# Down projection of 768 tokens by a recursion of seven block products, its sums made in the stage before

## The chip, the cores and the metric

The kernel runs on one core of a Trainium2 chip. The metric is the device time of one execution in microseconds; runs of the same kernel on the same chip are compared by their medians.

## The reference

One decoder layer for a prompt of 1024 tokens and 8 decode tokens that share the weights, all in float32. Columns are tokens: T = 1032. After the branches (RG-LRU, windowed attention, memory attention), a gated merge and an output projection with a layer norm, each token has a vector h of 1024 values. The last part of the layer is

```python
h = layer_norm(ALPHA * x + merged @ w_out, ln1_g, ln1_b)
gt, up = jnp.split(h @ w_gate_up, 2, axis=-1)        # 1024 -> 2 x 2816
h = layer_norm(ALPHA * h + (jax.nn.silu(gt) * up) @ w_down, ln2_g, ln2_b)   # 2816 -> 1024
```

The change is about the last line's product with w_down, 2816 x 1024.

## The kernel before, in words

Every tile has 128 partitions. 2816 = 22 x 128 gives NF = 22 "rows" f of the inner dimension, 1024 = 8 x 128 gives 8 output tiles m. A float32 operand is split into a high part (a cast to fp32r, on ACT) and a low part (the rest, a subtraction on DVE): `split`, lines L81 and L82. A product of two such pairs takes three matmuls, high x high, high x low and low x high, all accumulated in one PSUM bank.

**Gate and up stage** (`units`, `unit_step`). Two of the 22 rows are computed directly (`direct_units`); the other 20 rows are units. A unit multiplies the 2x2 blocks of (gate, up) weights with the 2x2 blocks of h by a recursion of seven products instead of eight: steps i = 0 to 6. The weight sums are made by VectorE just ahead (`fast_quarter`, L284, three steps ahead of TensorE), the sums of h once before (`h_sums`, tiles h_, t). A step is 24 matmuls of 258 columns: 4 row tiles x 3 x 2 halves p. Banks: fb (three rooms of tag mm), fd (t), fc (s). Evictions: ACT copies (L1188, L1190), then VectorE (L1192, L1195, L1197, L1199, L1200, L1202) and a tanh (L1198) make the activated row ft, and SP stores it to DRAM, tensor scr_f (L1204). SP also loads the gate and up weights (wgu, L92) into six rooms of tag raw.

**Down stage** (`down`). The tokens are in three chunks CH: 384, 384 and 264 (256 prompt and 8 decode tokens). For each chunk and each output tile m, `streamed` runs over the 22 rows: weights wdn are loaded by SP in pieces of four tiles, split (wd_h, wd_l), and used in three matmuls per row (L1244, L1245, L1246) into a bank dl. The rows are read back from scr_f by POOL's queue (`rows`, L1253, tiles gl and gh) and split. The first twelve rows of the first chunk are multiplied for four output tiles before the rest. Each finished bank is added to ALPHA x residual by VectorE (L1300, tile acc), summed for the mean, and the layer norm of a chunk (`layer_norm`, L961 to L977) runs in steps beside the next chunk's products (`norm_step`, at the output tiles in NORM_AT). The third chunk ends in `last_layer_norm`, which is the end of the kernel; its outputs o_y are stored by SP (L1290).

**Order.** The program is written as one stream; a list scheduler sets the order on each engine's queue, by readiness in its own model of times and then by place in the program. Each engine executes its queue in order. Memory of a closed pool is used again by the next one, and an instruction that writes there waits for the last user of the old tile.

Of the kernel before, what the change touches and what calls it, by code (L numbers as in the profile page):

```python
# [10 lines left out]
F32 = mybir.dt.float32  # L11
# [7 lines left out]
P = 128  # L19
# [5 lines left out]
CH = ((0, 384), (384, 384), (768, 264))  # L25
# [4 lines left out]
DIRECT_AT = ((0, 258), (258, 258), (516, 252), (768, 264))  # L30
ROOMS = (*range(83, 67, -1), *range(36, 4, -1), *range(67, 36, -1), *range(4, -1, -1))
EARLY, EARLY_ROWS = ("mm", "s", "mm", "s"), 12
# [26 lines left out]
class Builder:  # L59
# [218 lines left out]
    def fast_quarter(self, st, i):  # L278

        nc, ((a11, a12), (a21, a22)), u = self.nc, st["raw"], st["u"]  # L280
        if i in (1, 2, 4, 5):
            src = self.w1.tile([P, D // 2], F32, tag="sum", name=f"us{u}_{i}", bufs=self.sums)
# [659 lines left out]
    def col_mean(self, s, n, name):  # L942

        nc = self.nc
        hi = self.ph.tile([P, 384], F32R, tag="lh", name=f"{name}h", bufs=1)[:, :n]
        lo = self.ph.tile([P, 384], F32R, tag="ll", name=f"{name}l", bufs=1)[:, :n]
        self.split(hi, lo, s)
        ps = self.bank("o", f"{name}p")[:, :n]
# [4 lines left out]
    def layer_norm(self, c, r, s1, gcol, emit, name, late=False):  # L953
# [5 lines left out]
        mu = self.col_mean(s1, n, f"{name}mu{c}")  # L959
        s2 = ph.tile([P, 384], F32, tag="s2", name=f"{name}s2{c}", bufs=1)[:, :n]  # L960
        for m in range(KT):  # L961
            nc.vector.tensor_sub(r[m], r[m], mu)
            sq = s2 if m == 0 else ph.tile([P, 384], F32, tag="sq", name=f"{name}sq{c}_{m}", bufs=2)[:, :n]
# [5 lines left out]
        var = self.col_mean(s2, n, f"{name}va{c}")  # L969
        rs = ph.tile([P, 384], F32, tag="s2", name=f"{name}rs{c}", bufs=1)[:, :n]  # L970
# [20 lines left out]
    def last_layer_norm(self, n, r, product, gcol, emit):  # L991
# [4 lines left out]
        tile_ = lambda tag, name, bufs, dt=F32: ph.tile([P, 384], dt, tag=tag, name=name, bufs=bufs)[:, :n]  # L996
        s1, s2 = tile_("s1", "ls1", 1), tile_("s2", "ls2", 1)
        hi, lo = (ph.tile([P, n], F32R, tag=f"c0{e}", name=f"c0{e}", bufs=1) for e in "hl")
        e1, e2 = self.bank("t", "le1")[:, :n], self.bank("t", "le2")[:, :n]
# [13 lines left out]
        for m in range(KT):  # L1013
            ps = product(m, last=m < LATE)
# [6 lines left out]
            if m == 1:  # L1021
                s = tile_("xres", "lc0", 3)
                nc.vector.tensor_add(s, r[0], r[1])
                self.split(hi, lo, s)
            elif m == LATE - 1:
                with self.tc.issue_after(self.last_mm):
                    c0 = self.bank("o", "c0")[:, :n]
# [11 lines left out]
        mu, rs = tile_("xres", "lmu", 3), tile_("gt", "lrs", 3)  # L1039
# [481 lines left out]
```

## Time and profile before

| | |
|---|---|
| median of 3 runs | 1949.3 us (1948.71 to 1951.92) |
| span of the profiled execution | 1949.3 us, clock 0.997 |
| gate and up units | about 1280 to 1682 us |
| down, chunks of 384 tokens | 1682 to 1866.5 us |
| down, chunk of 264 tokens | 1866.5 to 1935 us |
| tail | 1935 to 1949.3 us |

In the profile, a busy time is a union of instruction times; matmuls overlap, so their distance of starts, not their duration, is what one costs. DVE is VectorE, ACT ScalarE, PE TensorE, POOL GpSimd and SP the queue that issues most DMAs. An "idle before" is charged to what ended the wait.

### The profile page before, as it was taken

The page shows a single profiled execution, that of the slowest core. Times are in us where ns is not written, and L with a number is a line of the kernel's source. Part 1 is how long each engine was busy: PE and PEld are TensorE (multiplying, and loading weights), DVE is VectorE, ACT ScalarE, POOL GpSimd, SP SyncE. Part 2 cuts the span into 40 slices and gives each one's busy share as a digit, 9 for nine tenths or more (in the row PEclk, how much of TensorE's full clock was granted, in tenths as well). Part 3 has the DMA queues.
Part 4 walks back from the last instruction along what each step waited for, and adds up shares of the span by engine and source line. Part 5 has one row for each costly group of instructions (what it writes and reads, how often), then busy time and mean ns, then how long its engine had stood idle before and what let it go on. Part 6 is the DMA issues. An engine that isn't in the chain of part 4 may idle for free. (4 is left out here: it accounts for less than half of the span.)

```text
span 1949.3 us, 37970 instructions
## 1 busy us (share of the span) xinstructions
PE 1912.5 (98%) x14356; PEld 1880.8 (96%) x14356; DVE 1364.0 (70%) x2875; ACT 1013.5 (52%) x2198; POOL 141.9 (7%) x218
## 2 busy tenths in 40 slices
PE   8999999999999999999999999999999999999997
PEld 8999999999999999989999999999999999999997
DVE  8678887888777555379877557976565665757566
ACT  5465565465556445378775245643333333635444
POOL 1000000000011200012210000000000000402002
PEclk9999999999999999999999999999999999999999
DMA  7444545365323866567534341122222222846554
GB/s 231 145 164 147 171 166 183 128 216 168 130 90 137 275 213 206 156 169 221 157 88 154 118 142 44 45 75 99 78 87 88 87 82 71 279 131 190 155 159 139
DMA packets 170919, 281.92 MB, mean 145 GB/s; under 512 B 20864, under 2 KB 85456, under 8 KB 170704
## 3 DMA queue, kind: packets, MB, share of 16 engines
q1 hardware_dynamic: 165840, 264.72, 43.0%
q0 software_dynamic: 4896, 14.78, 2.3%
q8 instruction: 112, 1.84, 0.4%
q14 instruction: 71, 0.58, 0.1%
HBM read 214.64 MB, written 66.85 MB: 144 GB/s over the span
## 5 line engine op out<-in xcount | busy, mean ns | idle before, releaser
L1246 PE MATMUL dl<-gh,wd_l 128*128 128x384 f32 (+1 forms) x528 | 167.4, 317 | 3.0 <-DVE wd_l L82 3.0
L1244 PE MATMUL dl<-gh,wd_h 128*128 128x384 f32 (+1 forms) x528 | 167.0, 317 | 1.0 <-ACT gh L81 1.0
L1245 PE MATMUL dl<-gl,wd_h 128*128 128x384 f32 (+1 forms) x528 | 167.2, 317 | 0.0
L1246 PEld LDWEIGHTS dl<-gh,wd_l 128*128 128x128 f32 x528 | 99.0, 188 | 3.5 <-DVE wd_l L82 3.5
L1244 PEld LDWEIGHTS dl<-gh,wd_h 128*128 128x128 f32 x528 | 98.9, 188 | 1.3 <-ACT gh L81 1.3
L1245 PEld LDWEIGHTS dl<-gl,wd_h 128*128 128x128 f32 x528 | 99.0, 188 | 0.5 <-DVE gl L82 0.5
L1253 POOL DMA_DIRECT2D gl<-scr_f x66 | 35.6, 540 | 789.0 <-PE fb L1179 630.8
L81 ACT CAST u_1h<-us 128x512 fp32r<-128x512 f32 x48 | 29.8, 621 | 87.6 <-issue 43.5
L592 ACT ACTIVATE bp<-bp,bst 128x257 f32<-128x257 f32 (+1 forms) x128 | 62.8, 493 | 18.0 <-DVE bst L588 17.7
L284 DVE TENSOR_TENSOR us<-ur,ur 128x512 f32<-128x512 f32 x96 | 66.0, 688 | 5.0 <-DMA ur<-win 2.9
L81 ACT CAST u_2h<-us 128x512 fp32r<-128x512 f32 x48 | 29.7, 619 | 76.5 <-PE fb L1179 38.2
L284 DVE TENSOR_TENSOR us<-us,ur 128x512 f32<-128x512 f32 x96 | 66.2, 689 | 2.3
L82 DVE TENSOR_TENSOR u_6l<-ur,u_6h 128x512 fp32r<-128x512 f32 x48 | 33.0, 688 | 43.8 <-PE fb L1180 28.5
L115 PE MATMUL brs<-bsH,wbs_h 128*128 128x384 f32 (+1 forms) x192 | 61.0, 319 | 1.0 <-ACT bsH L81 1.0
L82 DVE TENSOR_TENSOR u_4l<-us,u_4h 128x512 fp32r<-128x512 f32 x48 | 33.0, 687 | 40.1 <-PE fb L1180 29.1
L116 PE MATMUL brs<-bsL,wbs_h 128*128 128x384 f32 (+1 forms) x192 | 61.0, 318 | 0.0
L117 PE MATMUL brs<-bsH,wbs_l 128*128 128x384 f32 (+1 forms) x192 | 60.9, 317 | 0.0
L588 DVE CUSTOM_DVE_ANT_0 bp<-bs,mask,nsnk 128x256 f32<-128x256 f32 (+1 forms) x128 | 54.7, 458 | 3.3 <-PE bs L585 2.2
L82 DVE TENSOR_TENSOR u_5l<-us,u_5h 128x512 fp32r<-128x512 f32 x48 | 33.1, 690 | 30.0 <-PE fd L1180 14.6
L1198 ACT ACTIVATE ft<-za 128x516 f32<-128x516 f32 x40 | 25.5, 636 | 52.4 <-DVE za L1197 52.0
L81 ACT CAST u_5h<-us 128x512 fp32r<-128x512 f32 x48 | 30.0, 625 | 38.2 <-DVE us L284 24.7
L81 ACT CAST u_0h<-ur 128x512 fp32r<-128x512 f32 x48 | 29.8, 621 | 38.1 <-PE ub L301 19.2
(2019 smaller groups left out, 8112.7 us busy)
## 6 DMA issues: line engine op xcount, KB each, us to landing
ur<-win SPq DMA_DIRECT2D x112, 256.0 KB
ur<-wgu SPq DMA_DIRECT2D x80, 256.0 KB
scr_f<-ft SPq DMA_DIRECT2D x40, 258.0 KB
gl<-scr_f POOLq DMA_DIRECT2D x44, 192.0 KB, 4.8
dck<-cmk SPq DMA_DIRECT2D x32, 256.0 KB
dcv<-cmvT SPq DMA_DIRECT2D x32, 256.0 KB
st<-scr_q SPq DMA_DIRECT2D x32, 256.0 KB
scr_g<-za SPq DMA_DIRECT2D x10, 516.0 KB
```

Of the source, the lines that this page charges most:

```text
L81: ins = self.nc.scalar.copy(hi, src).ins
L82: self.nc.vector.tensor_sub(lo, src, hi.bitcast(F32))
L115: nc.tensor.matmul(ps, sh, mh, start=i == 0, stop=False)
L116: nc.tensor.matmul(ps, sh, ml, start=False, stop=False)
L117: self.last_mm = nc.tensor.matmul(ps, sl, mh, start=False, stop=closes and i == last).ins
L284: nc.vector.tensor_add(src, a, b)
L588: nc.vector.tensor_tensor_reduce(pg[g], s[:, u * 256:u * 256 + n], msk, 1.0, snk[:, g:g + 1], ALU.add, ALU.min, st[:, g:g + 1])
L592: nc.scalar.activation(x, x, AF.Exp, bias=st[:, g:g + 1], scale=-1.0, accum_out=st[:, 4 + g:5 + g])
L1244: nc.tensor.matmul(ps, sh, mh, start=k == 0, stop=False)
L1245: nc.tensor.matmul(ps, sh, ml, start=False, stop=False)
L1246: self.last_mm = nc.tensor.matmul(ps, sl, mh, start=False, stop=closes and k == NF - 1).ins
L1253: self.nc.gpsimd.dma_start(lo.bitcast(F32), self.scf[f][:, t0:t0 + n])
```

## The change

- The chunks become 384, 390 and 258 for the branch and output projections, and four equal pieces of 258 for the two direct rows. `h_sums` pairs tokens so that half p of a unit holds 516 consecutive tokens; a unit's store to scr_f is then contiguous.
- For the down product the tokens are two halves of 516; the first 384 of each half are the two token blocks of a 2x2 recursion, the last 132 of each half (NC) make one chunk of 264 that is multiplied directly as before. The other 2x2 is over the weights: rows f below and above 11 (KD), output tiles 2j and 2j + 1. Seven products, in the order DOWN_ORDER, each over four pairs j and eleven rows, in pieces of 4, 4 and 3 tiles (DOWN_PIECES).
- Four of the seven products need weight sums and four need row sums. They are made during the gate and up stage: `down_sums` (16 jobs of loads, four adds, stores to scr_w; one job every fourth step) and `row_sums` (once per unit f >= 11; two rows read back from scr_f, two taken from the unit's own ft, four subtractions, stores to scr_s). Both use a pool xs of four scratch tiles.
- In `down`, seven products replace the 16 (chunk, m) products of the two 384 chunks. Four banks b and four banks c hold running sums: products 0, 2, 4, 6 go into b and 3, 1, 5 into c without being cleared where a product adds to an earlier one. A bank is added to or subtracted from the residual after each product (`evict`).
- The norm of the second token block runs beside product 6, that of the first beside the last chunk. Low parts of the unsummed weights of products 0, 3 and 6 stay in memory (KEPT) and are used again for three quarters of the last chunk's weights, where only the high part is cast anew.

```diff
-CH = ((0, 384), (384, 384), (768, 264))
+CH = ((0, 384), (384, 390), (774, 258))
...
+KD = NF // 2
+NA = 384
+NC = T // 2 - NA
+DOWN_ORDER = (0, 3, 2, 1, 5, 4, 6)
+DOWN_PIECES = ((0, 4), (4, 4), (8, 3))
+SUM_PIECES = ((0, 3), (3, 3), (6, 3), (9, 2))
+KEPT = (0, 3, 6)
...
+    def down_sums(self, j, e):
+        nc = self.nc
+        o, n = SUM_PIECES[e][0] * P, SUM_PIECES[e][1] * P
+        a11, a12, a21, a22 = (self.scratch(f"dw{j}{e}{x}", n) for x in range(4))
+        for x, a in enumerate((a11, a12, a21, a22)):
+            at = (x % 2) * KD * P + o
+            nc.sync.dma_start(a, self.io["wdn"][2 * j + x // 2][:, at:at + n])
+        nc.vector.tensor_add(a22, a21, a22)
+        nc.vector.tensor_add(a21, a11, a21)
+        nc.vector.tensor_add(a11, a22, a11)
+        nc.vector.tensor_add(a12, a11, a12)
+        for i, a in ((1, a22), (4, a21), (2, a11), (5, a12)):
+            nc.sync.dma_start(self.scw[j][:, SUM_AT[i], o:o + n], a)
+    def row_load(self, k):
+        x = [self.scratch(f"rx{k}{h}", NA) for h in range(2)]
+        for h in range(2):
+            self.nc.sync.dma_start(x[h], self.scf[k][:, h * HT:h * HT + NA])
+        return x
+    def row_sums(self, k, early, st):
+        nc = self.nc
+        x00, x01 = early
+        x10, x11 = st["t", 0][:, :NA], st["t", 1][:, :NA]
+        t1, t4 = (self.scratch(f"rs{k}{x}", NA) for x in range(2))
+        nc.vector.tensor_sub(t1, x00, x01)
+        nc.vector.tensor_sub(x01, x11, x01)
+        nc.vector.scalar_tensor_tensor(x00, x01, -1.0, x00, op0=ALU.mult, op1=ALU.subtract)
+        nc.vector.scalar_tensor_tensor(t4, x00, -1.0, x10, op0=ALU.mult, op1=ALU.subtract)
+        for i, a in ((1, t1), (4, x01), (2, x00), (6, t4)):
+            nc.sync.dma_start(self.scs[k][:, ROW_AT[i] * NA:(ROW_AT[i] + 1) * NA], a)
...
             self.unit_step(st[f], i)
+            if n % 4 == 0 and jobs:
+                self.down_sums(*jobs.popleft())
+            if i == 3 and f >= KD:
+                early = self.row_load(f - KD)
             if i == 6:
+                if f >= KD:
+                    self.row_sums(f - KD, early, st[f])
                 del st[f]
...
+        for n, i in enumerate(DOWN_ORDER):
+            ahead = deque(range(KD))
+            nxt = [None] * KD
+            for j in range(KT // 2):
+                opens = i in (0, 1, 3)
+                if opens:
+                    tag = ("mm", "mm", "mm", "o")[j] if i == 0 else "st"[j % 2]
+                    banks["b" if i == 0 else "c", j] = self.bank(tag, f"dl{i}_{j}")[:, :NA]
+                ps = banks["b" if i in (0, 2, 4, 6) else "c", j]
+                mm = partial(nc.tensor.matmul, ps, skip_group_check=not opens)
+                for e, (k0, nk) in enumerate(DOWN_PIECES):
+                    wh, wl = self.down_weights(i, j, e)
+                    for k in range(k0, k0 + nk):
+                        w = slice((k - k0) * P, (k - k0 + 1) * P)
+                        xh, xl = act[k]
+                        mm(wh[:, w], xh, start=opens and k == 0, stop=False)
+                        mm(wh[:, w], xl, start=False, stop=False)
+                        self.last_mm = mm(wl[:, w], xh, start=False, stop=k == KD - 1).ins
+                    if ahead:
+                        k = ahead.popleft()
+                        if i == 6:
+                            last[k] = self.last_row(k)
+                        else:
+                            nxt[k] = self.down_row(DOWN_ORDER[n + 1], k, "ba"[n % 2])
+                    if i == 6 and (j, e) in ((0, 2), (1, 1), (2, 0), (2, 2)):
+                        self.norm_step()
+                evict(i, j, ps)
+            act = nxt
+            if i == 4:
+                norm_of(1)
+        norm_of(0)
+        for f in range(KD, NF):
+            last[f] = self.last_row(f)
```

More of the change, by code (lines that the diff above doesn't have):

```diff
@@ L24 @@
 T = TP + NB
-CH = ((0, 384), (384, 384), (768, 264))
+CH = ((0, 384), (384, 390), (774, 258))
+CW = 390
 NM = 256
@@ L1013, in last_layer_norm @@
         for m in range(KT):
-            ps = product(m, last=m < LATE)
+            ps = view(product(m, m < LATE))
             if m in NORM_AT:
@@ new lines, in rooms @@
+    def rooms(self):
+        side = lambda x, ks: [(f"{x}{2 * k + e}", NA) for k in ks for e in range(2)]
+        low = lambda i, js: [(f"k{i}{j}{e}", DOWN_PIECES[e][1] * P) for j in js for e in range(3)]
+        for tag, n in (low(0, (0, 1)) + low(6, (0, 1, 2)) + low(0, (2, 3)) + side("a", range(8, KD)) + low(6, (3,))
+                       + low(3, range(4)) + side("b", range(KD)) + [("pad", 64)] + side("a", range(8))):
+            self.gd.tile([P, n], F32R, tag=tag, name=f"room_{tag}", bufs=1)
@@ new lines, in down, with emit_to, emit @@
+        self.norm, self.lows = None, {}
+        self.rooms()
+        at = (0, HT)
+        r = [[a[:, o:o + NA] for a in self.accs] for o in at]
+        act = [self.down_row(DOWN_ORDER[0], k, "a") for k in range(KD)]
+        banks = {}
+        s1 = [ph.tile([P, CW], F32, tag=f"s1{x}", name=f"o2s{x}", bufs=1)[:, :NA] for x in range(2)]
+        done = [[], []]
+        def emit_to(dst):
+            def emit(m, v, scale=1.0):
+                nc.scalar.activation(v, v, AF.Identity, bias=self.vec[:, V_B2 + m:V_B2 + m + 1], scale=scale)
+                nc.sync.dma_start(dst(m), v)
+            return emit
@@ L1307, in build @@
+        tail = lambda a: a.rearrange("p (q n) -> p q n", q=2)
+        rows = [tail(a)[:, :, NA:] for a in self.accs]
+        self.last_layer_norm(2 * NC, rows, product, V_G2, emit_to(lambda m: tail(io["o_y"][:, m, :])[:, :, NA:]), tail)
     def build(self):
```

218 lines of the change are left out of this document (125 added, 93 removed).

## The prediction

> **What bounds the kernel now.** I read the page first, then its stretches of the second half, then who waited for whom on TensorE.
>
> ```profile
> span 1949.3 us, 37970 instructions
> PE 1912.5 (98%) x14356; PEld 1880.8 (96%) x14356; DVE 1364.0 (70%) x2875; ACT 1013.5 (52%) x2198; POOL 141.9 (7%) x218
> ```
>
> ```profile
> 1272.00:1477.00 205.00, 204.36 (x1706) 204.15 (x1706) 127.74 (x241) 78.02 (x156) 0.00 (x0) 1.00 0.26 84
> 1477.00:1682.00 205.00, 203.31 (x1697) 202.90 (x1695) 123.95 (x235) 77.29 (x154) 11.38 (x21) 1.00 0.33 106
> 1682.00:1774.00 92.00, 92.00 (x528) 91.48 (x529) 57.92 (x111) 47.16 (x98) 20.13 (x38) 1.00 0.61 190
> 1774.00:1866.50 92.50, 92.50 (x536) 92.50 (x535) 57.59 (x106) 43.39 (x84) 4.11 (x8) 1.00 0.55 164
> 1866.50:1935.00 68.50, 65.45 (x539) 64.83 (x538) 50.86 (x92) 36.91 (x71) 6.20 (x6) 1.00 0.55 164
> 1935.00:1949.30 14.30, 2.38 (x13) 1.71 (x12) 7.60 (x14) 5.69 (x12) 3.91 (x5) 0.76 0.22 76
> ```
>
> The columns after the length are PE, PEld, DVE, ACT and POOL busy, granted clock, DMA share, GB/s. TensorE is the bound in every stretch but the last 14.3 us: the gate and up stage (to 1682), the two down passes of 384 tokens (to 1866.5) and the pass of 264 all run at the full clock, with VectorE 60 to 75% busy beside it. TensorE's waits in the two stages are short (total us, times, longest; the first row is gate and up, the others down):
>
> ```profile
> PE fb L1180 <- DVE u_0l L82: 1.3, 2, 0.6
> ```
>
> ```profile
> PE dl L1246 <- DVE wd_l L82: 3.0, 2, 2.2
> PE dl L1244 <- ACT gh L81: 1.0, 1, 1.0
> ```
>
> So a matmul less is worth its full pitch, and work added elsewhere is free until it makes TensorE wait.
>
> **The matmuls removed.** The 768 tokens took 2 passes x 8 output tiles x 22 row tiles x 3 = 1056 matmuls of 384 columns; the recursion takes 7 products x 4 x 11 x 3 = 924. Removed: 132. Busy times overlap, so the price is the distance of starts:
>
> ```profile
> 1829.71 0.33 PE L1246 MATMUL dl<-gh,wd_l 128*128 128x384 f32 x1
> ...
> 1830.23 0.33 PE L1246 MATMUL dl<-gh,wd_l 128*128 128x384 f32 x1
> ```
>
> Three matmuls in 0.52 us, 0.1733 each (the two passes, 184.5 us over 1056 and the norm's 4, give 0.174). 132 x 0.1733: **-22.9 us**. The Trainium skill ("TensorE: Matmul & The Clock Gate", Back-to-back issue gap) puts the gap of a lone warm matmul at N/2.4 + 2.5 ns, 162.5 ns for 384 columns; the estimate by it would be -21.4 us, and the trace's longer pitch decides.
>
> The last 264 tokens keep their 528 matmuls. Chunk widths 390 and 258 replace 384 and 264 in the branch and output projections: equal sums, and a pitch nearly linear in columns (0.12 at 258 in the rows of fb below against 0.1733 at 384, 0.42 ns a column), so **0**. This is TensorE's own time and nothing would cover a difference.
>
> **The sums in the gate and up stage.** 16 jobs of down_sums (four loads, four adds, four stores, one job every fourth step) and 11 of row_sums (two loads, four subtractions, four stores). Twelve jobs have 384 columns, four have 256. VectorE's price for 512 and 384 columns, and the end of a unit on VectorE and on TensorE:
>
> ```profile
> 1681.30 0.68 DVE L82 TENSOR_TENSOR wd_l<-wd_0r__22005,wd_h 128x512 fp32r<-128x512 f32 x1
> 1681.95 2.43 DVE L82 TENSOR_TENSOR gl<-gl,gh 128x384 fp32r<-128x384 f32 x5
> ```
>
> ```profile
> 1637.79 0.70 DVE L1199 SCALAR_TENSOR_TENSOR ft<-ft,za 128x516 f32<-128x516 f32 x1 [0.71 <-ACT ft L1198]
> ...
> 1640.28 0.42 DVE L1202 SCALAR_TENSOR_TENSOR ft<-fb,ft 128x258 f32<-128x258 f32 x1
> ```
>
> ```profile
> 1640.53 0.28 PE L1178 MATMUL fb<-H_0h,u_0h 128*128 128x258 f32 x1
> ...
> 1641.98 0.28 PE L1178 MATMUL fb<-H_0h,u_0h 128*128 128x258 f32 x1
> ```
>
> Five of 384 take 2.43, so 0.47 each (0.35 at 256 in proportion); one of 512 takes 0.65 to the next start. Jobs: 48 x 0.47 + 16 x 0.35 = 28 us over the first 64 of 140 steps; a step is 24 matmuls, twice the 1.45 between the two rows of fb, so 64 steps are 186 us, and VectorE goes there from 62 to 77%. Row sums: 44 x 0.47 = 21 us over the last 220 us, 60 to 70%. The nearest row for such a load is the projection, which runs the same seven products:
>
> ```profile
> 300.00:600.00 300.00, 298.58 (x2455) 297.11 (x2455) 235.02 (x459) 173.53 (x334) 18.84 (x20) 1.00 0.45 152
> ```
>
> VectorE is at 78% and TensorE idle 0.5%, which over 402 us is 2 us against the 1.3 of now. The tight place is the unit's end: the eviction of the first fb bank ends at 1640.70, and the second half of the next unit's first step, which opens that bank again, starts at 1641.98: 1.3 us of cover, with VectorE nearly full before it. Two adds fit, three don't. I take **+1.5**, nearest to the projection's row; ends 0 and 8 (0.4 at each of 20 units).
>
> SP carries 128 + 66 more DMAs, and already waits for VectorE most of this stage:
>
> ```profile
> SPq L92 <- DVE us L284: 145.2, 33, 6.4
> SPq L1204 <- DVE ft L1200: 119.8, 19, 19.2
> ```
>
> That is 265 of 410 us. A sum's store that waits for its add (2 us for a job) holds back the wgu loads queued behind it, but the six raw rooms let those run up to a unit, 20 us, ahead of use: **0**; with that lead gone each would cost its landing. The bytes (w_down read and its sums written, 11.5 MB each, rows 4.3 and 8.7: 36 MB over 400 us, 90 GB/s beside 84 to 106) stay near the 152 that the projection moved. The contiguous scf store and the strided view in h_sums move the same columns under TensorE: **0**, and a few 0.1 us if they came on the path.
>
> **The seam at 1682.**
>
> ```profile
> 1680.64 0.28 PE L1180 MATMUL fb<-h_3h,u_6l 128*128 128x258 f32 x1
> 1681.97 0.62 PE L1244 MATMUL dl<-gh,wd_h 128*128 128x384 f32 x2 [1.05 <-ACT gh L81]
> ```
>
> ```profile
> L1253 POOL DMA_DIRECT2D gl<-scr_f x66: 536/538/595, 1662.9 to 1856.4; - x66
> DMA to landing us min/median/max: 2.7/4.3/5.4
> ```
>
> TensorE waits 1.05 us for the first cast rows, and will again: eleven rows come early as twelve did. New is a room. By the sizes in the code the kept low parts of product 0's first weights lie where the scratch of the sums lay, and the last unit's row_sums store from it. The last three subtractions follow the last eviction (three times 0.47, done near 1682.8), then SP's stores land. The trace shows no landing of an SP store; POOL's row loads took 2.7 to 5.4, so the first low parts can be written at about 1686 to 1688. Two of three matmuls don't need them: 22 of the first output pair (3.8 us, to 1685.8), and the two rows above show the order bent in this way (two L1244 in a row). I take **+2**, ends 0 and +5 (no bending). The Trainium skill ("DMA: Bandwidth & Descriptors", Latency and other measured facts) speaks of about 2 us fixed cost for a DMA; by that estimate the low parts come near 1685 and the term is 0. No run here shows it yet.
>
> **The seven products.** Per product of 22.9 us VectorE splits 12 weight pieces (4 x (0.65 + 0.65 + 0.47) = 7.1) and 11 rows (5.2) and evicts 4 banks, with a sum after the later ones (4 x 1.0 = 4): 16 of 22.9, 71% where it was 63, so hidden. ACT makes as many casts (half busy now), POOL 11 DMA issues of 0.54: hidden. Product 6 has norm(1) beside it:
>
> ```profile
> L976 DVE SCALAR_TENSOR_TENSOR acc<-acc,vec,n2rs 128x384 f32<-128x384 f32 x16 | 9.0, 613 | 0.0
> L966 DVE TENSOR_TENSOR n2s<-n2s,n2sq 128x384 f32<-128x384 f32 x14 | 7.7, 550 | 0.0
> L974 DVE RECIPROCAL n2rs<-n2rs 128x384 f32<-128x384 f32 x2 | 5.1, 2554 | 0.7 <-ACT n2rs L971 0.7
> L1300 DVE SCALAR_TENSOR_TENSOR acc<-acc,dl 128x384 f32<-128x384 f32 x9 | 5.0, 551 | 1.5 <-PE dl L1246 1.5
> L962 DVE TENSOR_TENSOR acc<-acc,n2mu1p 128x384 f32<-128x384 f32 x8 | 4.0, 548 | 0.0
> ```
>
> L1300 is an eviction, the others the norm, halved where a row holds two: 4.5 + 3.9 + 2.6 + 4.0 and two splits of 0.47, 16 us. With 7.1, 4 for evictions and about 3.9 for the last chunk's first rows that is 31 us in 22.9. The five rooms of high parts put the weights four pieces (8 us) ahead, and m = 0 of the last chunk needs no low part split, so most of the 8 us too much slides. **+1.5**, ends 0 and 8. Rows 11 to 21 of the last chunk use the rooms that product 6 frees only in its last quarter: POOL issue 0.54, landing 4.3, two casts of 0.5, against 4 us until they are due: **+0.5**, ends 0 and 2.
>
> **The last chunk.** Now TensorE waits 3.0 us for low parts there (the row of L1246 above; the one below is part of it). Three quarters of those splits go: 36 pieces, some 20 us of the 50.9 that VectorE works in 68.5. **-2**, ends -3 and 0.
>
> ```profile
> 1911.07 0.39 PE L1246 MATMUL dl<-gh,wd_l 128*128 128x264 f32 x1 [0.88 <-DVE wd_l L82]
> ```
>
> **The tail.** Same instructions over two runs of 132; o_y leaves in runs of half the length: **+0.4**, ends -0.5 and +1.
>
> Sum: -22.9 + 1.5 + 2 + 1.5 + 0.5 - 2 + 0.4 = -19.0. The profiled span is 1949.3, equal to the median of the three runs; nothing shown lies around it. 1949.3 - 19.0 = **1930.3 us**.
>
> **The rivals.** (1) Slower than before: VectorE takes a job's first add from its queue before the loads have landed. Nothing behind it runs, the unit's-end chain among it. Price: a landing of at least 2.7, plus the four adds (1.9), less the cover of 1.3, is 3.3 a job; 16 jobs give 53, so 1930 + 53 = 1983. It decides from 19/16 = 1.2 us a job. For it: every load is written right before its adds, with four scratch rooms. Against: the adds that wait for loads now lost 0.4 us to them in the whole stage:
>
> ```profile
> L284 DVE TENSOR_TENSOR us<-ur,ur 128x512 f32<-128x512 f32 x39 | 27.0, 691 | 1.5 <-DMA ur<-wgu 0.4
> ```
>
>  (2) The seam and product 6 cost their upper ends, +5 and +8 instead of 3.5: 1940. For it: 31 us of work in 22.9. Against: the order bends, and the next m is light. (3) Nothing of the added work shows: only -22.9 and the last chunk's -2 to -3 remain, 1924. For it: the projection's 0.5%. Against: the room at the seam. (4) The change doesn't do what it says: the seven products wait for sums from memory and lose the 22.9 again, 1949. Against: the sums lie written hundreds of us before, and rows come one product ahead.
>
> **How the numbers follow.** Forecast 0.66, rival 1 0.06, rival 2 0.14, rival 3 0.11, rival 4 0.03. The range runs from 1924 to 1941: rivals 2 and 3 in it, 1 and 4 out, 0.91 less the edges. The likeliest case alone: 1925 to 1936. The runs spread by 3 us, 0.2%, which is also the bound of what counts as a change. Faster 0.91, within 0.2% 0.04, slower 0.05, since rival 1 in a mild form ends at no change.
>
> **What would show it.** 924 matmuls of 384 columns at 0.173 from the seam to the last eviction of product 6, some 160 us against 184.5; TensorE's waits in gate and up at 1 to 3 us with VectorE near 77%; at the seam a wait for wd_l after 20 to 30 matmuls; a wait for VectorE late in product 6 or at the start of the last chunk, and none near its fourth output tile. The forecast is wrong if VectorE's waits in gate and up name a DMA, if fb waits for L1202 at each unit, or if the pitch of 384 columns is not 0.173 in the recursion.

## The result, and the profile after

The changed kernel takes 1996.5 us (median) against 1949.4 us for the kernel before on the same chip: a ratio of 1.0229, interval 1.0213 to 1.0245. It is slower by 47 us where 19 less were predicted. The four runs of the kernel after lie between 1987.6 and 1997.9 us. One run of `spread_pool` below, 2288.5 us at a granted clock of 0.751, was in a slower state than all others and is left out of its median. The head of the page of the kernel after, with the granted clock of the 40 slices (tenths, 9 is 90% or more):

```profile
span 1994.6 us, 38194 instructions
PE 1912.1 (96%) x14224; PEld 1878.3 (94%) x14224; DVE 1405.6 (70%) x2980; ACT 1019.9 (51%) x2219; POOL 159.5 (8%) x251
PEclk9999999999999999999999999999999999899988
```

TensorE has 132 matmuls less and is busy as long as before. Where that comes from is seen by stages: gate and up, the seven products, the last 264 tokens, the tail. First the kernel after, then two rows of the kernel before (PE, PEld, DVE, ACT, POOL busy, granted clock, DMA share, GB/s):

```profile
1278.00:1715.00 437.00, 415.79 (x3364) 413.09 (x3362) 293.16 (x567) 150.91 (x304) 8.13 (x16) 0.97 0.51 164
1716.00:1900.00 184.00, 166.84 (x937) 165.39 (x938) 127.08 (x241) 90.93 (x184) 43.07 (x76) 0.94 0.64 200
1900.00:1980.00 80.00, 67.53 (x534) 67.11 (x533) 35.11 (x71) 44.29 (x89) 10.73 (x13) 0.91 0.56 168
1980.00:1994.60 14.60, 2.07 (x11) 1.41 (x9) 7.61 (x14) 5.69 (x12) 3.91 (x5) 0.65 0.26 74
```

```profile
1276.60:1681.00 404.40, 403.05 (x3362) 402.42 (x3360) 246.23 (x464) 152.24 (x304) 11.38 (x21) 1.00 0.29 95
1682.00:1935.30 253.30, 250.25 (x1601) 249.12 (x1602) 166.38 (x307) 127.47 (x251) 30.43 (x51) 1.00 0.57 173
```

The length less PE's busy time is TensorE's idle time. In gate and up it goes from 1.35 to 21.2 us, and the same 3360 matmuls take 415.8 busy us instead of 403.05, at a granted clock of 0.97 instead of 1.00. Down (seven products and last tokens) goes from 253.3 to 264.0 us: idle from 3.05 to 29.6, busy from 250.25 to 234.4. The removed matmuls should have taken 22.9 of those busy us, so 7.0 came back as slower pitch. The sum: +19.9 idle and +12.7 slower pitch in gate and up, +26.6 and +7.0 in down, -22.9 for the matmuls, and some 2 us at the borders: 45.3, the difference of the spans.

Who TensorE waited for, kernel after, first in gate and up, then from the seam on (total, times, longest):

```profile
PE fb L1187 <- DVE ft L1211: 12.0, 5, 4.5
PE fb L1189 <- DVE u_0l L90: 4.7, 2, 2.9
PE fd L1187 <- ACT u_1h L89: 3.4, 2, 2.4
...
PE dl L1408 <- DVE gl L90: 12.2, 1, 12.2
PE dc L1434 <- ACT wl_0h L1339: 10.6, 1, 10.6
PE n2mu1p L957 <- ACT n2mu1h L89: 4.2, 1, 4.2
PE dc L1436 <- DVE wl_0l L90: 1.9, 1, 1.9
```

L1211 is the eviction chain at a unit's end, which the prediction named as a sign that rival 1 is right (L1202 before). What VectorE itself waited for in gate and up:

```profile
DVE dw L1225 <- DMA dw<-wdn: 16.4, 8, 4.0
...
DVE us L292 <- DMA ur<-wgu: 11.1, 4, 3.4
```

One such wait in order of time: SyncE's issues, VectorE, TensorE, kernel after (start, length):

```profile
1294.30 2.49 SPq L1224 DMA_DIRECT2D dw<-wdn  x3
...
1297.56 0.42 DVE L1206 TENSOR_TENSOR za<-fd,u2s 128x258 f32<-128x258 f32 x1
1300.15 0.56 DVE L1225 TENSOR_TENSOR dw<-dw,dw 128x384 f32<-128x384 f32 x1 [2.17 <-DMA dw<-wdn]
1300.62 0.42 DVE L1209 TENSOR_TENSOR ft<-ft,zb 128x258 f32<-128x258 f32 x1
...
1304.39 0.39 PE L1187 MATMUL fb<-H_0h,u_0h 128*128 128x258 f32 x1 [3.38 <-DVE ft L1211]
```

The last of the job's loads is issued by 1296.8; 3.4 us later the first add can start. It is at the head of VectorE's queue, so the unit's end chain (L1209, L1208, L1211) stands behind it, then is interleaved with the other three adds, and TensorE stands 3.4 us for the bank. Of the 21.2 idle us, 11.9 are four waits of this kind: TensorE starts again at 1304.4, 1349.0, 1372.9 and 1467.0, each time behind a first add that had waited for its load.

The rest is not all the same. Two lines of VectorE, kernel after, and one row of what SyncE's queue waited for:

```profile
1419.49 0.69 DVE L292 TENSOR_TENSOR us<-ur,ur 128x512 f32<-128x512 f32 x1 [3.34 <-DMA ur<-wgu]
...
1549.76 0.56 DVE L1247 SCALAR_TENSOR_TENSOR rs<-rx,ft 128x384 f32<-128x384 f32 x1
1550.23 0.68 DVE L90 TENSOR_TENSOR u_0l<-ur,u_0h 128x512 fp32r<-128x512 f32 x1
```

```profile
SPq L1230 <- DVE ft L1209: 27.5, 6, 17.6
```

At 1551.0 TensorE had waited 2.9 us for the low part u_0l, which stands right behind four subtractions of `row_sums` that waited for nothing; at 1415.5 it was 1.8 us, behind four adds that waited for nothing either. At 1420.9 it had waited 2.5 us for weights whose sum on VectorE (L292) stood 3.34 us for a late load: SyncE could issue these loads only from 1412.6 on, since a store of the sums (L1230) had held the queue for 17.6 us. That store waited for its add on VectorE, which ends at 1412.2; the row names the instruction beside it.

At the seam, kernel after, VectorE and then TensorE:

```profile
1724.95 0.69 DVE L90 TENSOR_TENSOR wk<-wd_0r,wd_0h 128x512 fp32r<-128x512 f32 x1 [7.64 <-DMA scr_s<-rx]
...
1728.12 2.43 DVE L90 TENSOR_TENSOR gl<-gl,gh 128x384 fp32r<-128x384 f32 x5
1728.73 0.69 PE L1408 MATMUL dl<-gl,wd_0h 128*128 128x384 f32 x1 [12.17 <-DVE gl L90]
...
1731.13 0.52 PE L1409 MATMUL dl<-gh,wk 128*128 128x384 f32 x1
1731.45 0.52 PE L1407 MATMUL dl<-gh,wd_0h 128*128 128x384 f32 x1
...
1733.24 0.33 PE L1407 MATMUL dl<-gh,wd_1h 128*128 128x384 f32 x1
1733.41 0.33 PE L1408 MATMUL dl<-gl,wd_1h 128*128 128x384 f32 x1
```

The first kept low part waits 7.64 us for the last stores of the row sums to leave the scratch on which its room lies. The row splits (gl), whose first eight rows ScalarE had cast by 1719.0, stand behind it and behind four more low parts: 12.2 us. After that TensorE's pitch is 0.32 us until 1731.8 and then 0.17 again.

ScalarE's queue at the start of the last tokens, kernel after:

```profile
1909.76 0.41 ACT L89 CAST ghc<-glc 128x264 fp32r<-128x264 f32 x1 [2.32 <-DMA glc<-scr_f]
1910.76 0.79 ACT L89 CAST ghc<-glc 128x264 fp32r<-128x264 f32 x2 [0.58 <-DMA glc<-scr_f]
1912.70 0.41 ACT L89 CAST ghc<-glc 128x264 fp32r<-128x264 f32 x1 [1.16 <-DMA glc<-scr_f]
1913.01 0.61 ACT L1339 CAST wl_0h<-wl_0r 128x512 fp32r<-128x512 f32 x1
```

All casts of rows 11 to 21 stand ahead of the next weight's cast (wl_0h), which needs nothing of them. The wait of 4.2 us in product 6 is the same picture: the cast that opens norm(1) starts at 1876.92, behind a cast that waited for its row until 1876.61.

**The theory** after this: mainly one mechanism, at three places. An instruction that depends on a transfer stands in an engine's in-order queue close behind that transfer's issue, the transfer lands 2 to 8 us later, and independent work behind it stops. **Rivals:** VectorE is too full with the adds; the added traffic is too much; SyncE's queue, where stores wait for adds, holds back the units' own weights.

### The profile page after: what moved, and what is told of

Read it like the earlier page. It is cut to its first block, busy times and chain, and to the rows that moved or that the text cites. A ratio compares the mean times of both kernels' runs of the same rounds, so it can differ in the third digit from the quotient of the medians.

```text
span 1994.6 us, 38194 instructions
## 1 busy us (share of the span) xinstructions
PE 1912.1 (96%) x14224; PEld 1878.3 (94%) x14224; DVE 1405.6 (70%) x2980; ACT 1019.9 (51%) x2219; POOL 159.5 (8%) x251
## 3 DMA queue, kind: packets, MB, share of 16 engines
q8 instruction: 111, 1.82, 0.4%
## 4 chain that ended last, share of the span: by engine, by line
PE 70%; issue 8%; DMA 8%; DVE 8%; ACT 5%; POOL 1%; SPq 0%; POOLq 0%; ACTq 0%; DVEq 0%
PE ub L308 4%; PE ub L309 4%; PE ub L310 4%; PE fb L1187 3%; PE fb L1189 3%; PE fb L1188 3%; PE ud L309 2%; PE ud L308 2%; PE ud L310 2%; PE fd L1189 2%; PE fd L1187 2%; PE fd L1188 2%; PE brs L124 2%; PE brs L123 2%; PE op L124 2%
## 5 line engine op out<-in xcount | busy, mean ns | idle before, releaser
L292 DVE TENSOR_TENSOR us<-ur,ur 128x512 f32<-128x512 f32 x96 | 66.0, 688 | 14.5 <-DMA ur<-wgu 11.1
L1291 POOL DMA_DIRECT2D gl<-scr_f x33 | 17.8, 539 | 691.8 <-DVE rs L1247 665.4
L292 DVE TENSOR_TENSOR us<-us,ur 128x512 f32<-128x512 f32 x96 | 66.2, 689 | 2.1
L123 PE MATMUL brs<-bsH,wbs_h 128*128 128x384 f32 (+2 forms) x192 | 61.2, 320 | 1.0 <-ACT bsH L89 1.0
L125 PE MATMUL brs<-bsH,wbs_l 128*128 128x384 f32 (+2 forms) x192 | 61.4, 320 | 0.0
L124 PE MATMUL brs<-bsL,wbs_h 128*128 128x384 f32 (+2 forms) x192 | 61.4, 320 | 0.0
L1408 PE MATMUL dl<-gl,wd_0h 128*128 128x384 f32 x112 | 39.0, 348 | 12.2 <-DVE gl L90 12.2
L90 DVE TENSOR_TENSOR gl<-gl,gh 128x384 fp32r<-128x384 f32 x77 | 40.0, 554 | 14.2 <-ACT gh L89 14.2
L90 DVE TENSOR_TENSOR u_4l<-us,u_4h 128x512 fp32r<-128x512 f32 x48 | 33.0, 688 | 21.7 <-PE fb L1189 10.4
L1199 ACT COPY p1s<-fb 128x258 f32<-128x258 f32 x40 | 14.9, 374 | 60.4 <-PE fb L1189 60.4
L1409 PE MATMUL dl<-gh,wk 128*128 128x384 f32 x132 | 45.2, 344 | 0.1
L89 ACT CAST gh<-gl 128x384 fp32r<-128x384 f32 x77 | 36.5, 511 | 16.8 <-DMA gl<-scr_s 13.4
L89 ACT CAST u_4h<-us 128x512 fp32r<-128x512 f32 x48 | 29.6, 618 | 29.1 <-PE fb L1188 11.8
```

The lines of the kernel that those rows point to most:

```text
L89: ins = self.nc.scalar.copy(hi, src).ins
L90: self.nc.vector.tensor_sub(lo, src, hi.bitcast(F32))
L123: nc.tensor.matmul(ps, sh, mh, start=i == 0, stop=False)
L124: nc.tensor.matmul(ps, sh, ml, start=False, stop=False)
L292: nc.vector.tensor_add(src, a, b)
```

## The experiments

The kernels below for which no ratio is given ran once. The kernel after itself ranges over 10 us, so a few us of a total say little there, and the argument goes by stages and waits.

**Parts of the sums.** `no_sums` drops `down_sums` and `row_sums`; `adds_only` keeps the arithmetic alone, `dma_only` the transfers alone.

```diff
 no_sums:    - self.down_sums(*jobs.popleft())   - self.row_sums(f - KD, early, st[f])
             - src = self.scw[j][:, SUM_AT[i], o:o + n]
             + src = self.io["wdn"][2 * j + i // 4][:, o:o + n]
 adds_only:  - nc.sync.dma_start(a, self.io["wdn"]...)   - nc.sync.dma_start(self.scw[j]..., a)
             + a11, a12, a21, a22 = (a[:, :n] for a in self.kept4)
 dma_only:   - nc.vector.tensor_add(a22, a21, a22)   ...   - nc.vector.tensor_sub(t1, x00, x01)   ...
```

> Left out: the sums of weights and rows in the gate and up stage; the products that read them are fed weight tiles and rows as they are, in the same number and shape, so the stage of down products keeps its instructions. Theory (adds and casts stand at the head of an in-order queue and wait for transfers that land late): the gate and up units come back from 437 us to that of the kernel before, 404 us (402 to 407), with no TensorE wait above 1.5 us; the first down product no longer waits for the 8.1 us store, so the wait of 12.2 us at the seam goes to under 3 us; the waits of 4.2 us (norm step in product 6) and 10.6 us (start of the last 264 tokens) stay, since nothing of theirs is touched. Total 1945 to 1953. Rival (the work in the down stage itself is slow, not the sums): units about 404 too, but the seam's wait stays above 8 us and the total is 1958 or more.

> Left out: the loads and stores of the sums; VectorE does the same 108 additions at the same places on four scratch tiles that were loaded once, and the down products read plain weights and rows. Theory: without transfers to wait for the additions fill VectorE's idle time; the units take 404 to 409 us, at most 5 more than before, and no VectorE wait for a transfer of a weight sum is left. Rival A (VectorE is too full with the added work): the units stay at 425 us or more. Rival B (traffic): units at 404 to 409 here too, and the next run carries the loss.

> Left out: the 108 additions; the scratch tiles are loaded and stored as they are, the same number of transfers of the same sizes in the same queue, and the down products read what was stored. Theory (VectorE's queue waits for landings): with no addition that waits, VectorE has nothing at its queue's head that stands for a load; the units take 404 to 412 us. Rival B (the transfers themselves, by bandwidth or by SyncE's queue in which stores and loads of scratch stand ahead of the unit weights): the units stay at 425 us or more, with VectorE's sums of unit weights waiting for their own loads.

Measured: 1949.2, 1958.7 and 1960.9 us (before: 1951.0). The rows of gate and up, in that order (three kernels):

```profile
1275.60:1679.70 404.10, 402.83 (x3362) 402.17 (x3360) 246.18 (x462) 152.76 (x305) 8.22 (x16) 1.00 0.27 89
```

```profile
1278.30:1684.50 406.20, 403.49 (x3362) 402.33 (x3361) 291.77 (x568) 153.50 (x304) 8.13 (x15) 1.00 0.27 91
```

```profile
1277.60:1688.40 410.80, 405.77 (x3362) 404.11 (x3361) 243.27 (x462) 151.97 (x304) 8.16 (x16) 1.00 0.54 175
```

404.1, 406.2, 410.8, and 437.0 with both. VectorE with all its additions (291.8 us busy, like the 293.2 of after) costs 2 us, the transfers 7; the other 24 us exist only where additions and transfers meet, so neither VectorE's load nor the traffic alone is the cause of most of it. One caution: without loads to wait for the scheduler orders VectorE's queue anew, and in `adds_only` the row sums no longer stand right ahead of u_0l, so the 2 us do not cover the wait at 1551. `no_sums` shows something else: without the sums the time is hardly below that of the kernel before (1951.0 in this comparison), because the waits in down remain, 8.5 us at the start of the last tokens and 4.4 in product 6 among them.

**The seam alone.** `rooms` lays out the same rooms in another order, so that not product 0's but product 3's low parts lie on the scratch.

```diff
- low(0, (0, 1)) + low(6, (0, 1, 2)) + low(0, (2, 3)) + side("a", range(8, KD)) + low(6, (3,)) + low(3, range(4)) ...
+ low(3, range(4)) + low(6, (3,)) + low(0, range(4)) + side("a", range(8, KD)) + low(6, (0, 1, 2)) ...
```

> Only the order in which the rooms of the down stage are laid out is changed: the kept low parts of the first product no longer lie on the scratch of the row sums, those of the second product do. Theory: the first product's low parts wait only for tiles that were read some microseconds before the seam; the wait of 12.2 us there goes to 3 us or less, the slow matmul pitch behind it goes with it, and the time falls by 10 to 14 us, to 1982 to 1987; the units stay at 437 us, the waits of 4.2 and 10.6 us stay. Rival (first product waits for its own weight or row loads, the store being only the last of several that land together): the wait stays above 8 us and the time falls by less than 4 us.

Measured: 1990.6 us, 6 less than after: between the two, and by its total not clear of the range of the kernel after. By stages it is clear: down takes 256.1 us where it took 264, the units 439.6, some 2.6 more than after. TensorE's longest wait at the seam, and the row of down:

```profile
PE dl L1408 <- DVE gl L90: 4.2, 1, 4.2
```

```profile
1718.00:1974.10 256.10, 236.68 (x1471) 234.80 (x1472) 161.93 (x311) 135.50 (x272) 53.81 (x89) 0.95 0.64 196
```

VectorE no longer waits for the stores, so they were the cause of 8 of the 12.2 us. The other 4.2 are order: in this run's VectorE queue the last row sums and five low parts (1719.11 to 1722) still stand ahead of the first row split.

**The start of the last tokens.** `last_early` multiplies rows 0 to 10 for four output tiles before any row from 11 on, and queues each row's cast apart from its load.

```diff
-    self.split(hi, lo, dst)                      # right behind the row's load
+    self.loaded.append((hi, lo, dst))            # split_rows(n) later, issue_after(newest ScalarE instruction)
+    for m in range(4):
+        half(m, 0, True)                         # rows 0..10 of four tiles, four banks
+        if m: self.split_rows(4)
```

> Nothing is left out. For the last 264 tokens the first halves (rows 0 to 10) of four output tiles are multiplied ahead of the second halves, in four banks; casts of rows 11 to 21 are spread between them; in product 6 the casts of rows 0 to 10 stand three pieces behind their loads. Theory (ScalarE's queue has casts that wait for row loads at its head): the waits of 5.3 us (norm step in product 6) and 10.6 us (rows 11 to 21) go to 1.5 us or less each, the slow pitch after them goes too, and the time falls by 12 to 18 us, to 1979 to 1985. Rival (the rows land too late for any order, since GpSimd's loads wait for rooms that product 6 still reads): at least 6 us of the 10.6 stay, and the time falls by less than 8 us.

Measured: 1983.3 us, 13 less, as the theory had it; down takes 250.1 us, 14 less, and the units 437.2, as in the kernel after. The 10.6 and 4.2 us are gone from TensorE's waits; what remains of them:

```profile
PE dc L1452 <- ACT wl_0h L89: 1.6, 1, 1.6
```

**Additions later in VectorE's queue.** `adds_late` queues a job's additions three unit steps behind its loads (`issue_after` puts an instruction behind another one of the same engine, with no wait for it).

```diff
+    yield                                        # resumed when n % 4 == 3
+    with self.tc.issue_after(self.newest(mybir.EngineType.DVE)):
         nc.vector.tensor_add(a22, a21, a22)
```

> Nothing is left out. The four additions of each weight job stand three unit steps (about 9 us) later in VectorE's queue than the job's loads are issued, instead of as early as they may; loads, stores and the number of additions stay. Theory (the head of VectorE's queue waits for landings of 3.5 to 5 us, and the stores behind the additions hold SyncE's queue): the units fall from 437 us to about that of the run with transfers but without additions, 411 us (406 to 416), and the time to 1968 to 1978. Rival (transfers and additions together, by shared SBUF traffic or too many semaphores, slow each other wherever the additions stand): the units stay above 428 us.

Measured: 1984.0 us; units 424.6, between the theory's 406 to 416 and the rival's 428. Half of the excess over `dma_only` goes, not all. Of what is left, one wait of VectorE and one of SyncE's queue (total, times, longest):

```profile
DVE dw L1230 <- DMA dw<-wdn: 14.5, 7, 7.0
...
SPq L1235 <- DVE dw L1230: 48.5, 13, 17.7
```

A store stands 17.7 us in SyncE's queue for a later addition, as one stood 17.6 in the kernel after, and the units' own weight loads and the next job's loads stand behind it. The 7.0 us wait follows from it: that job's loads are issued from 1401.0 to 1403.5, and its first add starts at 1407.6.

**The other queue.** `pool_queue` issues the sums' loads and stores from GpSimd and leaves the additions where they were.

```diff
- nc.sync.dma_start(a, self.io["wdn"]...)      - nc.sync.dma_start(self.scw[j]...)
+ nc.gpsimd.dma_start(a, self.io["wdn"]...)    + nc.gpsimd.dma_start(self.scw[j]...)
```

> Nothing is left out. The loads and stores of both kinds of sums are issued from GpSimd's queue instead of SyncE's; the additions stand where they stood in the scheduler's terms. It parts the two queues: if the loss in the units comes from SyncE's queue (stores that wait for additions hold back the loads of the units' own weights), it goes, and the units take 405 to 415 us. If it comes from VectorE's queue alone (additions that wait for their loads), it stays, and the units take 428 us or more. My theory has both in it, the second as the larger: 418 to 432 us.

Measured: 2018.5 us; units 462.4, far above my 418 to 432. The case of VectorE's queue alone (428 or more) holds by its number, but there the loss was to stay, and it grew by 25 us. VectorE's waits of this kernel, and then 18 us of its queue in order of time:

```profile
DVE dw L1225 <- DMA dw<-wdn: 59.7, 14, 6.9
```

```profile
1430.41 0.56 DVE L1225 TENSOR_TENSOR dw<-dw,dw 128x384 f32<-128x384 f32 x1 [5.41 <-DMA dw<-wdn]
...
1448.59 0.56 DVE L1225 TENSOR_TENSOR dw<-dw,dw 128x384 f32<-128x384 f32 x1 [6.76 <-DMA dw<-wdn]
```

Three jobs follow one another in VectorE's queue (the one between at 1439.49, after 6.53 us), and TensorE stands 22.7 us. With the sums' transfers out of SyncE's queue no sum of unit weights waits for its load any more (11.1 us in the kernel after), while the waits for job loads go from 16.4 to 59.7 us and the loss is larger. So SyncE's queue isn't the main cause; the head of VectorE's queue is. How much SyncE's queue had cost is not shown, because GpSimd's queue brings waits of its own: its stores stood up to 7.3 us for an add, its loads up to 4.5 us for the stores of the job before.

**Together, and refined.** `all3` joins `rooms`, `adds_late` and `last_early`. `spread` also moves the jobs off two steps and queues product 0's low parts behind the row splits; `spread_pool` is the same with the weight jobs' transfers in GpSimd's queue.

```diff
 spread:       - if n % 4 == 0 and jobs:     + if n in (*range(0, 36, 4), *range(38, 66, 4)):
               + with self.tc.issue_after(row_lo[...]): wh, wl = self.down_weights(i, j, e)
 spread_pool:  - nc.sync.dma_start(a, ...)   + nc.gpsimd.dma_start(a, ...)
```

> Nothing is left out. The three edits together: other order of rooms, additions three steps later, rows of the last 264 tokens early. Theory (the lost time is separate waits that add up): from 1996.5 us, 24 to 28 us less in the units, 6 at the seam, 12 to 18 in product 6 and the last 264 tokens: 1944 to 1954. Were all waits gone with nothing in their place it would be near 1930, the predicted time. Rival (the waits cover for each other, so the gains don't add up): 1960 or more.

> Nothing is left out. The three edits of the run before, and two more: the 16 weight jobs leave out the two steps around step 36, where two jobs' additions stood behind one another and a store held SyncE's queue for 17.7 us; and in the first down product the weights' low parts are queued behind the row splits that are used before them. Loads and stores stay in SyncE's queue. Theory: the waits of 2.6 and 6.6 us at step 42 and their slow pitch go, the units fall from 424 to 408 to 415 us; the wait of 4.1 us at the seam falls under 2; the time goes from 1960.6 to 1943 to 1952. Rival (SyncE's queue of loads behind stores is itself the rest of the loss): the units stay above 418 us, and only the next run is faster.

> Nothing is left out. The same, with the weight jobs' loads and stores issued from GpSimd's queue, so that no load of the units' own weights stands behind a store that waits for additions (the additions now stand three steps behind their loads, unlike in the earlier run with GpSimd's queue). Theory: both queue heads are free of late landings; the units take 405 to 409 us and the time is 1938 to 1946, faster than the kernel before (1950). Rival (GpSimd's transfers slow VectorE, or the traffic itself costs): the units stay above 415 us.

Measured: 1960.6 (ratio to before 1.0044, 1.0028 to 1.0061), 1959.5 (1.0048, 1.0033 to 1.0062) and 1957.5 us (1.0050, 1.0030 to 1.0070). `all3` is 36 us below after. Its total lies in the rival's case (1960 or more), but the rival's reason does not hold: by stages `adds_late` had 12 us less in the units and `rooms` and `last_early` 8 and 14 less in down, and `all3` has 12.7 less in the units (424.3) and 25 less in down (239.1), so the gains do add up. My 1944 to 1954 was too low because it counted on 24 to 28 us from the units. The two refinements failed against forecasts of 408 to 415 and 405 to 409: units at 424.2 and 421.5. In `spread` a store still holds SyncE's queue 17.7 us, and in `spread` and `spread_pool` VectorE still waits 10.4 and 22.7 us for job loads. The four scratch tiles are part of it: loads of a job wait for the stores of the job before, up to 6.6 us at a time in `spread`. More scratch was not tried. Down in `spread`, from the seam to the last matmul (the 239.1 of `all3` are the shortest of any run):

```profile
1701.40:1941.40 240.00, 232.01 (x1470) 229.51 (x1471) 160.66 (x311) 133.53 (x273) 53.92 (x89) 0.99 0.67 209
```

Against 253.3 before that is 13.3 us of the 22.9: 8.0 us are idle where 3.05 were, and the pitch still takes 4.7 of the rest back (232.0 against 250.25 - 22.9 = 227.35).

**GpSimd makes the sums.** In `pool_adds` GpSimd loads, adds and stores the weight sums; the row sums stay VectorE's, with their transfers in GpSimd's queue. In `pool_all` the row sums of units 11 to 20 are GpSimd's too.

```diff
- nc.vector.tensor_add(a22, a21, a22)     + nc.gpsimd.tensor_add(a22, a21, a22)
 pool_all:
- self.row_sums(f - KD, early, st[f])     + self.rows_late(f - KD)   # 4 loads, 5 operations, 4 stores on GpSimd
```

> Nothing is left out. The weight sums are made by GpSimd, which has nothing else to do in the units: its queue issues a job's loads, does the four additions and issues the stores, so neither VectorE's nor SyncE's queue holds anything that waits for them. Loads and stores of the row sums go through GpSimd's queue too (but for the last one); with it the other order of rooms, the order at the seam and the early first halves of the last 264 tokens. Theory (what costs is an instruction at the head of a busy queue that waits for a landing, and not the work or the traffic): the units take 405 to 411 us, the time is 1935 to 1947, below the kernel before. Rival (VectorE is slowed by GpSimd's reads and writes of the same memory, or the chain of a job of some 12 us is too long for 16 of them to end before the first row sums): units above 415 us, 1950 or more.

> Nothing is left out. As the run before, but the row sums of units 11 to 20 are GpSimd's too: four loads, five additions or subtractions and four stores behind the weight jobs in its own queue, so that VectorE no longer holds a subtraction that waits for a row load behind 16 jobs (82.6 us of TensorE's time in the run before). Only the last unit's row sums stay with VectorE. Theory: the units take 405 to 412 us (404.3 before; 416 in the run before without that one wait), the down stage some 240 as in the runs with the other edits, against 253.6 before; the time is 1936 to 1946, faster than the kernel before. Rival (VectorE's operations become slower beside GpSimd's, 930 against 692 ns for the same operation in the run before, and units feel it): units 416 us or more, time 1950 or more.

Measured: `pool_adds` 2034.9 us. The first row sum stands at the head of VectorE's queue for a load that is queued on GpSimd behind the weight jobs (VectorE's, then TensorE's wait):

```profile
DVE rs L1247 <- DMA rx<-scr_f: 111.7, 11, 84.9
...
PE fd L1187 <- ACT u_1h L89: 82.6, 1, 82.6
```

One instruction at the wrong place costs 82.6 us of TensorE; of the 498.6 us of the units 416 are left without it. `pool_all` takes that away and takes 1953.2 us, a ratio of 1.0006 to before (0.9994 to 1.0017): no difference that can be measured, and the best of the versions with the recursion that leave nothing out. Its stages, one VectorE operation in 1300 to 1500, and two executions of that operation:

```profile
1278.20:1694.20 416.00, 405.76 (x3362) 402.83 (x3360) 280.22 (x460) 150.30 (x303) 239.41 (x334) 1.00 0.54 178
1696.00:1941.00 245.00, 234.78 (x1471) 232.33 (x1472) 162.18 (x315) 133.70 (x272) 56.88 (x94) 0.97 0.68 210
```

```profile
L292 DVE TENSOR_TENSOR us<-us,ur 128x512 f32<-128x512 f32 x20 | 18.4, 920 | 0.7
```

```profile
1327.76 0.69 DVE L292 TENSOR_TENSOR us<-us,ur 128x512 f32<-128x512 f32 x1
...
1345.33 1.53 DVE L292 TENSOR_TENSOR us<-us,ur 128x512 f32<-128x512 f32 x1
```

The units come to 416.0 us, in the rival's range in both forecasts: the sum of unit weights takes 920 ns on average, 691 before. The average hides two kinds: 14 of the 20 take 691 to 694 ns as before, six take 1379 to 1532, and each of these six, but none of the 14, has a GpSimd addition beside it (the one at 1345.33 an addition of 1.03 us that starts at 1345.28). The Trainium skill ("Trainium Architecture — The Big Picture", What this means for kernel authors) has VectorE and GpSimd share a port pair by an exclusive lock. These times, undisturbed or about doubled and nothing between, agree. No run separates what this costs the units from the traffic, which by itself cost 7 us. No version here beats the kernel before.

## Why the prediction was wrong, point by point

- **The matmuls removed, -22.9: right.** 924 matmuls of 384 columns, 0.173 us each where the clock is full (1733.24 to 1733.41). It isn't in the time, since waits and slower pitch took more than it gave.
- **The sums in gate and up, +1.5, ends 0 and 8: the step that failed**; they cost 32.6, 19.9 of them idle time of TensorE and 12.7 slower pitch. The reasoning by VectorE's load was right as far as it went: `adds_only` measures 2 us for it. Its own limit, that two adds fit at a unit's end and three don't, was passed at 1415.5 and 1551.0, for 4.7 us. The transfers alone cost 7 us in `dma_only`, at the step's upper end; 90 GB/s beside 84 to 106 is 174 to 196, not near 152, and 184 were measured from 1278 to 1480. What failed most is the price of a load that hasn't landed, which I left to rival 1 with a chance of 0.06. The row I set against it, adds that wait 0.4 us for loads, belonged to loads that are issued up to a unit ahead; the new jobs' loads are issued within one step, into scratch that the job before has only just stored. Rival 1 had the place (VectorE's head of queue, the unit's end), and its bound of 1.2 us a job was passed: 32.6 over 16 is 2.0. Its 53 us were too many: 11 of the 16 first adds waited (8 of them put down to their own loads), and only four made TensorE wait for the bank (11.9 us).
- **"SP carries 128 + 66 more DMAs ... 0": wrong in part.** VectorE's sums of unit weights wait 11.1 us for their loads, in `dma_only` up to 11.0 us at once; the lead of a unit was not there at all steps. In the kernel after this reached TensorE once, with 2.5 us at 1420.9. Whether that or the traffic is the 7 us of that run, no run separates.
- **The seam, +2, ends 0 and +5: right cause, wrong size**, 12.2 us. I had the room and the stores. The stores were waited for until 1724.95, 7.6 us after the last subtraction, not 3 to 5, and `rooms` shows that this is 8 of the 12.2; the other 4.2 are the order of the low parts ahead of the row splits. I let 22 matmuls run meanwhile, but the row splits that they need stood behind the waiting low part in the same queue. The estimate of 0 that the prediction drew from the Trainium skill ("DMA: Bandwidth & Descriptors", Latency and other measured facts) is further off: it took the fixed cost of about 2 us alone, and the trace has 7.6 us to the landing here.
- **Product 6 with its norm, +1.5, ends 0 and 8: inside, by luck**: 4.2 and 0.6 us, not for VectorE's 31 us of work but for a cast on ScalarE behind a row that hadn't landed.
- **Rows 11 to 21, +0.5, ends 0 and 2: wrong**, 10.6 us. I priced one row's way (issue, landing, two casts). Eleven rows come one after another as product 6 frees their rooms, and the weight's cast is queued behind the last of them.
- **The last tokens' relief, -2, ends -3 and 0: inside, half the size**; 1.9 us of the 3.0 remain, so 1.1 went. **The tail, +0.4: about right.** From the start of the last matmul of the products (1935.31 before, 1980.01 after) it goes from 14.0 to 14.6 us.
- **A term that was missing:** the slower pitch after most waits, 12.7 and 7.0 us (below).
- **A sum among the rivals:** rival 4, the forecast with the 22.9 us lost again, is 1953 by its own words, not 1949.

So the prediction failed at one assumption used four times, that work hidden by an engine's idle share stays hidden whatever order its queue has. `rooms`, `adds_late` and `last_early` change order and place alone; they take 8 us from down, 12 from the units and 14 from down. Open: how the last 12 to 20 us of the units divide between traffic, the remaining waits for loads and, in `pool_all`, VectorE's slower operations.

## What to carry to other kernels

An engine that is 70% busy has room for more work only if that work never waits at the head of its queue: for each added instruction that reads a transfer, ask how long after the issue it stands and what is behind it. Scratch that the turn before must first store holds the needed lead back, however idle the engines are; price it as landing plus work plus landing for each turn. And ask what stands right ahead of the work that the bound engine needs next: four additions that waited for nothing cost 1.8 and 2.9 us where they stood ahead of one split. When a recursion removes 20 us, lay out first what it must prepare, and time the preparation's transfers and its arithmetic apart, because each alone can be nearly free.

## What the hardware showed that was not expected

A wait of some 2 us can cost nearly twice its length, and another one of the same length nothing more. At 1372.93 TensorE had waited 1.82 us; the matmul pitch of 258 columns, 0.12 before, is about 0.21 from 1373.5 to 1376.9. At 1415.53 it had waited 1.82 us too, and the pitch stays at 0.12. The granted clock behind each of the two, kernel after:

```profile
1373.00:1376.00 3.00, 3.00 (x16) 3.00 (x17) 1.63 (x4) 0.38 (x1) 0.00 (x0) 0.59 0.80 261
...
1415.60:1418.60 3.00, 2.84 (x22) 2.62 (x22) 0.55 (x2) 0.50 (x2) 0.00 (x0) 1.00 0.94 307
```

In the first 3.0 us 16 matmuls run instead of 25: 1 us lost, and about 1.7 until the pitch is back. Six of the seven waits of 1.8 to 4.5 us in gate and up were followed by such a stretch, at a granted clock of 0.50: five stretches of 3.41 us and one of 6.83, 23.9 us in all with 1.4 of them idle. Half of the rest, 11.3 us, is nearly all of the 12.7 there. None followed the wait of 1.0 us (at 1556) or one of 1.86 us among the last tokens (at 1955.6). The six stretches begin at 1305.26, 1349.63, 1373.52, 1421.31, 1465.68 and 1551.02, whole multiples of 3.413 us apart (13, 7, 14, 13 and 25), so where a wait lies seems to count beside its length; no run here tests that. The Trainium skill ("TensorE: Matmul & The Clock Gate", What's actually happening) gives half clock after an idle window of about 3.4 us and full clock after as much activity. The stretches of 3.4 us agree with it; the waits of 1.8 to 2.9 us behind which the clock fell are shorter than that, so here the trace's bound is the one to plan with.

Transfers land at very different distances from their issue. The stores of the row sums at the seam, issued about 1717 together with GpSimd's loads of the next rows, were waited for until 1724.95, twice the 3.4 us that a job's load took at 1296.8. The DMA share was 0.90 at 319 GB/s from 1717 to 1725, and 0.76 at 212 GB/s from 1294 to 1300. That the traffic is the reason is not shown, since one case is stores and the other loads.
